# Hybrid decoder trunk on one core: three engines issue in the order of the text through the whole program instead of only in its first lines

## Chip, cores and metric

The kernel runs on one core of a Trainium2 chip. A core has a matrix engine (TensorE, PE in the profile), a vector engine (VectorE, DVE), a scalar engine (ScalarE, ACT), GpSimd (POOL) and SyncE (SP). Each takes its instructions from a queue of its own, in order, and they wait for one another by semaphores. In this kernel SP and POOL issue the DMAs. The metric is the device time of one execution in microseconds (us).

## Reference

One layer of a decoder trunk with two recurrent mixers beside each other, all in float32, for 1024 tokens of width 1024:

```python
mod = silu(c) @ ada_w + ada_b
shift, scale, gate = split(mod, 3)
h = rms_norm(x, norm_w) * (1 + scale) + shift
hq, hf, hi, hz, gq, gk, gv, gz, ga, mg = split(h @ w_in, IN_OFFSETS)
y_h = hgrn2_branch(hq, hf, hi, hz, lb, hgrn_norm_w)   # 8 heads, keys 128, values 128
y_g = gla_branch(gq, gk, gv, gz, ga, alpha_w, alpha_b, gla_norm_w)  # 4 heads, keys 128, values 256
mg = sigmoid(mg.reshape(B, T, 2, 1024))
merged = mg[:, :, 0] * (y_h @ w_branch[0]) + mg[:, :, 1] * (y_g @ w_branch[1])
x = x + gate * (merged @ w_out)
return rms_norm(x, final_norm_w)
```

Both mixers are gated linear attention: a state S of keys by values follows S_t = diag(a_t) S_(t-1) + k_t v_t^T, and the output is o_t = S_t^T q_t; the decay a_t is a gate of its own for each key channel. It is computed chunk by chunk: products of queries and keys inside a chunk, weighted by the decay between them, and the state between chunks. The GLA branch then takes a root mean square of each head, the HGRN branch one over all heads.

## The kernel before

All large products are made in three parts. A float32 operand is split into a rounded part `hi` (ScalarE, L193) and the remainder `lo` (VectorE, L196, for some GpSimd), and the product is hi·hi + lo·hi + hi·lo. Buffers in SBUF come from 46 slots of 128x1024 floats that the host hands out and takes back in a fixed order when it builds the program; PSUM has two double banks `pd`, one double bank `sc_ps` and two small banks `pm`.

The stages, in the order of the text:

- **Start.** `norm_x` (L204 to L208) normalizes the rows of x; TensorE transposes them (L215), ScalarE copies the result out (L217), and `make_h` (L224, then L193 and L196) applies shift and scale. Shift and scale come from `make_mod`, whose VectorE chains (L247, L251) and small products (L257, L259) read `ada_w` in five blocks. The first group of projections is made for the first half of the tokens while h comes out, one 128-row block `d` at a time (L349). Then the text has `make_ga` (L305), the eight transposes of the second half with their `make_h`, and `first_group`, which makes the second half's projections (L372).
- **Stream.** A list of projection jobs: `Feat` (L455, 48 products of 128x512 for 128 output features), `Vblk` and `Vblk2` (L514 to L516 and L557 to L559, values). Each job has a load (SP), a prep (the split of its weights, L193 and L196) and a run; its result leaves PSUM by a sigmoid and a product (L852, L853), by two sigmoids and three operations (L978 to L982) or by a copy (L519, L562). The class `Stream` calls a job's load and prep ahead of its run when slots are free.
- **Two tracks woven into the stream.** After every 6 products of a job, `weave` gives a bit of time to two queues of Python generators. The side track holds the attention of the heads, one after the other; the back track holds elementwise work for the last stages, mainly `weight_sums` (L1169 to L1173 with DMAs on POOL, L1175) and `factors` (L1138). A generator yields the number of 6-product units that should pass before its next step is put into the text. So the text is one sequence in which small steps alternate with groups of products.
- **Attention of a head** (`attention`, L571 on): builds of `xb` (ScalarE L589, VectorE L590 to L593); products of 16-wide pieces L597; VectorE L599 to L615, L624 and L625 with ScalarE L622 and L623; products L629; VectorE L631 to L635 and eight predicated copies L642 to L645; products L658, then VectorE L677, L678, L681, L684, and ScalarE L687; products L665, L677 and L678 again, ScalarE L692; products L671, L677 and L678, ScalarE L696; transposes L709, the states' products L731 with VectorE L737, the outputs' products L748 and L750. GLA heads close with `root_mean` (products L863 and L864, ScalarE L865) and, in four steps, a reciprocal L891 and two products L893 each.
- **Pair stage** (`last_stages`): four matrix products, each by seven products of half-size factors as in Strassen's scheme, for 4 groups b, in the order 1, 2, 5, 6, 3, 7, 4 of the products and over 4 `Pair` objects (L1293). Around them stand the splits of the weights (`prep_duo`, L1233 and L1234) and of the factors (`build`, L1211 to L1215), copies of a bank out of and back into PSUM (`snap_of` L1269 and L1271, `seed` L1276), sums (`summed`, L1280) and outputs.
- **Two output blocks** (L1076 to L1097).

What sets the order of issue: the text calls every instruction in one sequence, and dependences are turned into semaphores. Then a scheduler of the framework orders each engine's queue by its own model of the times, and it may put an instruction ahead of one that stands earlier in the text where no dependence forbids it. Within `tc.manual_schedule(engines=...)` the named engines keep the order of the text. The kernel opens this for PE, ScalarE and VectorE at L156 to L158, ahead of the first `vec_rows`:

```python
order = ExitStack()
order.enter_context(tc.manual_schedule(engines={
    mybir.EngineType.PE, mybir.EngineType.Activation, mybir.EngineType.DVE}))
vec_rows(rows_c, 8, R_C)
...
norm_x(0, x_t)
vec_rows(rows_a, 24, R_SH)
order.close()
make_mod(0, 1, mods.pop(0), 4)
```

It closes at L324, ahead of the first `make_mod`. Behind that line a handful of instructions are held by `tc.keep_in_program_order`, among them the first step of a `make_mod` chain and the first splits of the group's weights.

Of the kernel before, what the change touches and what calls it, by code (L numbers as in the profile page):

```python
# [83 lines left out]
def hybrid_trunk_kernel(  # L84
# [65 lines left out]
    def vec_rows(rows, n, at):  # L150
        pv = mtile()
        i = nc.tensor.transpose(pv[:, 0:n], rows, ident[0:n, 0:n])
        nc.vector.tensor_copy(vec[:, at:at + n], pv[:, 0:n])
        return i

    order = ExitStack()  # L156
# [84 lines left out]
    def make_mod(d0, nd, parts, on_pe):  # L241
        kq = 4 // nd
        acc = scT_f[:, (d0 // 2 % 2) * 512:(d0 // 2 % 2) * 512 + 2 * nd * P].rearrange("p (a f) -> p a f", a=2)
        for k in range(on_pe, KT):
            src = parts[k // kq][:, k % kq]
            if k == on_pe:
                i = nc.vector.tensor_scalar_mul(acc, src, cs[:, k:k + 1])  # L247
                if on_pe:
                    tc.keep_in_program_order(i)
            else:  # L250
                nc.vector.scalar_tensor_tensor(acc, src, cs[:, k:k + 1], acc, ALU.mult, ALU.add)  # L251
        pm = mtile()
        for half in range(2):
            for i in range(nd):
                o = pm[:, half * nd + i:half * nd + i + 1]
                for k in range(on_pe):
                    nc.tensor.matmul(o, parts[k // kq][:, k % kq, half, i * P:(i + 1) * P], cs[:, k:k + 1],  # L257
                                     start=(k == 0), stop=False)
                nc.tensor.matmul(o, acc[:, half, i * P:(i + 1) * P], one_t, start=(on_pe == 0), stop=True)  # L259
        S.free(*parts)  # L260
        nc.vector.tensor_add(modv[:, :, d0:d0 + nd], pm[:, 0:2 * nd].rearrange("p (a b) -> p a b", a=2),
                             vec[:, R_SH:R_SH + 16].rearrange("p (a b) -> p a b", a=2)[:, :, d0:d0 + nd])
        nc.vector.scalar_tensor_tensor(amul[:, d0:d0 + nd], modv[:, 1, d0:d0 + nd], 1.0,
                                       vec[:, R_NW + d0:R_NW + d0 + nd], ALU.add, ALU.mult)
# [56 lines left out]
        load_w(bi)  # L321
    norm_x(0, x_t)
    vec_rows(rows_a, 24, R_SH)
    order.close()  # L324
    make_mod(0, 1, mods.pop(0), 4)
    transpose_x(0, x_t, 0)
    transpose_x(0, x_t, 1)
# [1134 lines left out]
    make_m()  # L1462
    out0.run({1: out1.load, 3: out1.prep})
    out1.run({})


# [27 lines left out]
```

## Time and profile before

| | |
|---|---|
| runs | 1283.7, 1285.03, 1285.39 us |
| median | 1285.03 us |
| span of the profiled execution | 1279.6 us |
| TensorE busy | 1219.5 us (95%), 8603 instructions |
| VectorE busy | 802.6 us (63%), 1239 |
| ScalarE busy | 506.3 us (40%), 754 |
| GpSimd busy | 151.4 us (12%), 246 |

The profile gives the span from the first to the last instruction of the profiled execution; its time with what lies around the span is not given, and the median of the runs is 5.4 us above it. The page of the profile slices the span into 40 parts of 32 us with each engine's busy tenths; from the trace behind it come windows (busy time between two moments), groups of instructions by line, waits (which engine waited for what) and the timeline. A line such as `PE L455 MATMUL pd<-b,b` names the engine, the line of the text, the operation, what it writes and what it reads.

### The profile page before, as it was taken

Reading aid. Unit: us, or ns where it says so; the run is one execution under the profiler, and the core shown is the slowest. Engines: PE = TensorE matmul, PEld = TensorE weight load, DVE = VectorE, ACT = ScalarE, POOL = GpSimd, SP = SyncE. Lnnn points to the kernel's source line nnn. Section 1 sums busy time; section 2 is a strip of 40 time slices with the busy share of each in tenths; the row PEclk is TensorE's granted clock in tenths of the full one; section 3 lists DMA queues with packets and bytes.
Section 4 is the critical chain, followed back from the end, with each engine's and each line's share of the span. In section 5 each row is a group of like instructions: output and inputs, shape, how many; then the busy total and the mean of one; then the engine's idle time right before and its main releaser. Section 6 shows DMA issues by size and latency. Waiting matters only on the chain. (4 is left out here: it accounts for less than half of the span.)

```text
span 1279.6 us, 20905 instructions
## 1 busy us (share of the span) xinstructions
PE 1219.5 (95%) x8603; PEld 1002.3 (78%) x8603; DVE 802.6 (63%) x1239; ACT 506.3 (40%) x754; POOL 151.4 (12%) x246
## 2 busy tenths in 40 slices
PE   4899999999999999999999999999998999998997
PEld 3677899879797877787787878877786777776885
DVE  5746334785849475876874576686544555659643
ACT  4466612333333223323322233356544454364222
POOL 5510000101111121121220101011121000000000
PEclk9799999999999999999999999999999999999999
DMA  8733100654553266363272511336579846445402
GB/s 270 274 104 93 40 18 18 230 165 129 186 155 134 83 191 221 100 198 126 99 264 100 180 39 62 101 123 208 171 254 335 279 168 204 164 133 178 167 34 99
DMA packets 134129, 195.05 MB, mean 152 GB/s; under 512 B 7819, under 2 KB 97985, under 8 KB 134034
## 3 DMA queue, kind: packets, MB, share of 16 engines
q1 hardware_dynamic: 118114, 140.01, 34.9%
q0 software_dynamic: 15872, 53.70, 10.9%
q8 instruction: 67, 1.10, 0.3%
q14 instruction: 28, 0.23, 0.1%
q10 hardware_dynamic: 48, 0.01, 0.0%
HBM read 140.21 MB, written 53.48 MB: 151 GB/s over the span
## 5 line engine op out<-in xcount | busy, mean ns | idle before, releaser
L455 PE MATMUL pd<-b,b 128*128 128x512 f32 x1632 | 396.9, 397 | 0.0
L455 PEld LDWEIGHTS pd<-b,b 128*128 128x128 f32 x1632 | 301.1, 189 | 64.1 <-issue 1.2
L1293 PE MATMUL pd<-b,b 128*128 128x512 f32 x912 | 221.7, 395 | 12.6 <-ACT pd L1276 5.3
L1293 PEld LDWEIGHTS pd<-b,b 128*128 128x128 f32 x912 | 170.0, 189 | 55.0 <-ACT pd L1276 6.5
L196 DVE TENSOR_TENSOR b<-b,b 128x1024 fp32r<-128x1024 f32 (+1 forms) x95 | 101.0, 1072 | 69.4 <-ACT b L193 41.7
L193 ACT CAST b<-b 128x1024 fp32r<-128x1024 f32 (+1 forms) x95 | 84.6, 905 | 140.4 <-DMA ws<-b 16.8
L1293 PE MATMUL sc_ps<-b,b 128*128 128x512 f32 x432 | 108.6, 397 | 3.9 <-DVE b L1280 2.1
L1293 PEld LDWEIGHTS sc_ps<-b,b 128*128 128x128 f32 x432 | 81.2, 190 | 24.0 <-DVE b L1280 2.5
L1234 DVE TENSOR_TENSOR b<-b,b 128x1024 fp32r<-128x1024 f32 x56 | 68.0, 1222 | 45.3 <-ACT b L1233 28.6
L1233 ACT CAST b<-b 128x1024 fp32r<-128x1024 f32 x56 | 58.2, 1049 | 50.0 <-PE pd L1293 14.1
L514 PE MATMUL pd<-b,b 128*128 128x256 f32 x256 | 75.6, 295 | 0.0
L516 PE MATMUL pd<-b,b 128*128 128x256 f32 x256 | 72.5, 283 | 0.0
L515 PE MATMUL pd<-b,b 128*128 128x256 f32 x256 | 72.5, 283 | 0.0
L1175 POOL DMA_DIRECT2D ws<-b x64 | 35.3, 552 | 205.3 <-DVE b L1169 82.2
L1215 DVE TENSOR_TENSOR b<-b,b 128x1024 fp32r<-128x1024 f32 x36 | 43.4, 1220 | 25.5 <-ACT b L1214 14.1
L557 PE MATMUL pd<-b,b 128*128 128x512 f32 x128 | 51.9, 405 | 0.0
L1214 ACT CAST b<-b 128x1024 fp32r<-128x1024 f32 x36 | 37.6, 1050 | 35.2 <-PE pd L1293 10.0
L559 PE MATMUL pd<-b,b 128*128 128x512 f32 x128 | 50.2, 392 | 0.0
L558 PE MATMUL pd<-b,b 128*128 128x512 f32 x128 | 50.0, 390 | 0.0
L514 PEld LDWEIGHTS pd<-b,b 128*128 128x128 f32 x256 | 49.0, 191 | 0.5
L515 PEld LDWEIGHTS pd<-b,b 128*128 128x128 f32 x256 | 48.9, 191 | 0.6
L516 PEld LDWEIGHTS pd<-b,b 128*128 128x128 f32 x256 | 48.9, 191 | 0.0
(249 smaller groups left out, 1964.9 us busy)
## 6 DMA issues: line engine op xcount, KB each, us to landing
b<-in_w_in_dram SPq DMA_DIRECT2D x66, 512.0 KB, 4.0
ws<-b POOLq DMA_DIRECT2D x64, 256.0 KB, 3.1
b<-ws SPq DMA_DIRECT2D x32, 512.0 KB, 4.9
b<-in_x_dram SPq DMA_DIRECT2D x16, 512.0 KB, 6.7
b<-in_ada_w_dram SPq DMA_DIRECT2D x32, 256.0 KB, 6.0
b<-in_w_branch_dram SPq DMA_DIRECT2D x16, 512.0 KB, 4.8
b<-h SPq DMA_DIRECT2D x14, 512.0 KB, 4.3
b<-yg SPq DMA_DIRECT2D x14, 512.0 KB, 4.4
```

What stands on the lines that cost most here:

```text
L193: i = nc.scalar.copy(hi, src)
L196: (eng or nc.vector).tensor_sub(lo, src, hi.bitcast(F32))
L455: nc.tensor.matmul(ps[0:w, th * 512:(th + 1) * 512], a[:, k, 0:w], b[:, th * 512:(th + 1) * 512], start=(k == 0 and n == 0), stop=(k == KT ...
L514: nc.tensor.matmul(o, lh, hi[:, k % 4, :], start=(k == 0), stop=False)
L515: nc.tensor.matmul(o, lh, lo[:, k % 4, :], start=False, stop=False)
L516: nc.tensor.matmul(o, ll, hi[:, k % 4, :], start=False, stop=(k == KT - 1))
L557: nc.tensor.matmul(o, lh, hi[:, k % 2, :], start=(k == 0), stop=False)
L558: nc.tensor.matmul(o, lh, lo[:, k % 2, :], start=False, stop=False)
L559: nc.tensor.matmul(o, ll, hi[:, k % 2, :], start=False, stop=(k == KT - 1))
L1233: nc.scalar.copy(hi, t)
L1234: nc.vector.tensor_sub(lo, t, hi.bitcast(F32))
L1293: nc.tensor.matmul(o, a[:, sl], c, start=(p in (1, 5) and kt == 0 and n == 0), stop=(kt == 3 and n == 2), skip_group_check=True)
```

## The change

`order.close()` moves from L324 to the end of the kernel, behind the last output block. TensorE, VectorE and ScalarE then issue all their instructions in the order of the text; the queues of SP and POOL are still put in order by the scheduler. No instruction, buffer or dependence is added or taken away. Lines behind L324 have a number lower by one in the changed kernel.

```diff
     norm_x(0, x_t)
     vec_rows(rows_a, 24, R_SH)
-    order.close()
     make_mod(0, 1, mods.pop(0), 4)
     transpose_x(0, x_t, 0)
     transpose_x(0, x_t, 1)
...
     make_m()
     out0.run({1: out1.load, 3: out1.prep})
     out1.run({})
+    order.close()
```

## Prediction

> **What bounds the kernel now.** I read the page first, then windows by stage, TensorE's waits, and TensorE's timeline around the attention steps.
>
> ```profile
> span 1279.6 us, 20905 instructions
> PE 1219.5 (95%) x8603; PEld 1002.3 (78%) x8603; DVE 802.6 (63%) x1239; ACT 506.3 (40%) x754; POOL 151.4 (12%) x246
> PE   4899999999999999999999999999998999998997
> ```
>
> TensorE is busy in 1219.5 of 1279.6 us, so it is the bound, and no order of issue takes work off it: all that can be won is its idle time, 60 us, part of which is the start before any data is there. What can be lost has no such ceiling. The stages (start and end in us from the span's start, length, then busy time and instructions of PE, PEld, DVE, ACT and POOL, granted clock, DMA share, GB/s):
>
> ```profile
> 24.00:90.00 66.00, 58.85 (x254) 46.07 (x254) 41.80 (x63) 32.56 (x64) 25.26 (x28) 0.87 0.56 190
> 130.00:900.00 770.00, 756.82 (x6628) 635.73 (x6627) 515.30 (x857) 270.10 (x399) 93.36 (x127) 1.00 0.41 132
> 940.00:1185.00 245.00, 230.57 (x981) 184.36 (x981) 151.25 (x167) 119.64 (x158) 11.18 (x21) 0.99 0.64 214
> 470.00:485.00 15.00, 12.12 (x174) 9.55 (x174) 13.97 (x35) 3.25 (x4) 4.24 (x8) 1.00 0.62 209
> 584.11:587.52 3.41, 3.41 (x9) 2.64 (x10) 1.49 (x3) 0.67 (x1) 0.00 (x0) 0.50 0.32 86
> ```
>
> The 770 us from 130 to 900 hold the projections with the attention heads woven between them; TensorE idles there for 13.2 us in all. The pair stage (940 to 1185) idles for 14.4. VectorE has much to do beside both: 515 of 770 us, and 14.0 of 15 in the stretch at 470. So it has little slack where several of its pieces fall together.
>
> ```profile
> PE sc_ps L658 <- DVE blk L645: 6.8, 6, 2.5
> PE pd L1293 <- ACT pd L1276: 5.3, 3, 3.5
> PE pd L1293 <- DVE b L1234: 3.3, 2, 1.7
> ```
>
> These are TensorE's largest waits in those two stages (total, times, longest). In the attention they end on VectorE; in the pair stage on work that stands behind other work on ScalarE or VectorE.
>
> **The change part by part.** Nothing is added or removed: the same instructions, buffers and slots. Until now the scheduler brought each queue into an order of its own from the early lines on; afterwards PE, DVE and ACT follow the text, and only the DMA-issuing queues (SP, POOL) are still reordered. I matched the trace with the order in which the text calls the instructions. Some 650 of TensorE's 8603 records, 475 of ScalarE's and 885 of VectorE's come behind one that stands later in the text. So TensorE's queue is nearly the text's already (except for the attention's small steps, which the scheduler moved against the projection products), while VectorE's and ScalarE's are thoroughly different. What changes is that a DVE or ACT instruction that is ready no longer passes one that waits, and a split or a sum that is due much later stands where the text puts it, ahead of an attention step that TensorE will soon ask for.
>
> *Attention.* I walked the text head by head: how much TensorE work stands between one attention step and the next, and how much VectorE and ScalarE must do, in text order, in between. The fullest case is the last GLA head. First TensorE's present timeline (start, duration, line, count):
>
> ```profile
> 379.40 0.39 PE L864 MATMUL pm<-b,ones_r 128*128 128x512 f32 x1
> 383.95 8.38 PE L455 MATMUL pd<-b,b 128*128 128x512 f32 x36
> 392.26 1.31 PE L597 MATMUL sc_ps<-xb,b 128*32 128x80 f32 x64
> 393.51 7.09 PE L455 MATMUL pd<-b,b 128*128 128x512 f32 x30
> 400.53 0.89 PE L629 MATMUL sc_ps<-xb,b 128*32 128x48 f32 x64
> 401.35 4.37 PE L455 MATMUL pd<-b,b 128*128 128x512 f32 x18
> 406.35 0.73 PE L658 MATMUL sc_ps<-b,b 128*32 128x16 f32 x64 [0.63 <-DVE blk L645]
> ```
>
> Then the pieces of VectorE and ScalarE (busy, mean ns of one, idle before):
>
> ```profile
> L891 DVE RECIPROCAL b<-b 128x256 f32<-128x256 f32 x16 | 26.9, 1722 | 3.4 <-ACT b L865 3.4
> L893 DVE TENSOR_TENSOR b<-b,b 128x256 f32<-128x256 f32 x32 | 10.9, 403 | 0.0
> L1169 DVE TENSOR_TENSOR b<-b 128x512 f32<-128x512 f32 x16 | 11.0, 690 | 6.1 <-PE pm L748 2.8 <-PE pm L750 1.8 <-PE pd L455 0.9
> L591 DVE TENSOR_TENSOR xb<-b,b 128x512 f32<-128x512 f32 x12 | 13.4, 1119 | 0.0
> L593 DVE TENSOR_TENSOR xb<-xb,b 128x256 f32<-128x256 f32 x12 | 7.8, 649 | 0.1
> L853 DVE TENSOR_TENSOR b<-b,pd 128x1024 f32<-128x1024 f32 x24 | 29.4, 1223 | 11.9 <-ACT b L852 11.8
> L631 DVE TENSOR_TENSOR b<-xb,tot 128x768 f32<-128x768 f32 x12 | 12.0, 1001 | 0.0
> L644 DVE COPY_PREDICATED blk<-mask,sc_ps 128x64 f32<-128x64 int32 x24 | 5.5, 229 | 0.4
> L196 DVE TENSOR_TENSOR b<-b,b 128x1024 fp32r<-128x1024 f32 (+1 forms) x95 | 101.0, 1072 | 69.4 <-ACT b L193 41.7 <-PE pd L516 19.3 <-issue 3.2
> L677 DVE TENSOR_TENSOR b<-b,tot 128x512 f32<-128x512 f32 x36 | 24.8, 689 | 28.2 <-PE sc_ps L658 10.5 <-PE sc_ps L665 9.2 <-PE sc_ps L671 8.4
> L687 ACT COPY scT<-blk 32x256 f32<-32x256 f32 x48 | 19.3, 403 | 39.0 <-DVE blk L684 38.4
> L980 DVE TENSOR_SCALAR b<-b,oml,lb 128x1024 f32<-128x1024 f32 x8 | 6.5, 809 | 1.2 <-ACT b L978 1.1
> ```
>
> - At L597. Behind the root mean the text gives VectorE four reciprocals and eight products (4 x 1.72 + 8 x 0.40 = 10.1), four sums like L1169 (2.8) and the four builds L590 to L593 (between 0.65 and 1.12 each, 3.3): 16.2 us. TensorE arrives 12.9 us after the last L864 (392.26 less 379.40). The difference is 3.3; ScalarE's square root (L865) in front of the first reciprocal adds up to a microsecond, so 3 to 4.4, taken 3.9. Today the builds were done long before, ahead of the reciprocals.
> - At L629: 7.1 us of products against some 7.5 of VectorE: nothing.
> - At L658. VectorE has L853 (1.2), two sums (1.4), L631 to L635 (2.9: two of about 1.0, three small) and eight copies of about 0.2 (1.7): 7.2, against L629 and 18 products, 5.3: wait 1.3 to 2.3, taken 1.8.
> - At L665. Ahead of L677 the text has four splits L196 (4.3) and two sums (1.4); then L677 and its twin (1.4), two small ones (0.5), and ScalarE's four L687 (1.6): 9.2, against L658 and 18 products, 5.0: taken 4.2.
> - At L671. L980 to L982 stand ahead of the next L677 and wait for ScalarE's two gates behind the L687: some 5 us against L665 and 6 products (2.2): taken 2.7.
>
> Sum 12.6 for this head. The other GLA heads, walked alike: none for the first (nothing stands in front of it), 7 and 8 for the second and third (reciprocals and sums, but not the splits of a new block just there). The eight HGRN heads have no reciprocals; they wait where four splits of the next value block (4 x 1.07) fall between two steps, 5.1 and 3.3 in two heads, and 0 to 1.4 in the other six, 12.6 together. In all 12.6 + 15 + 12.6 = 40; the present idle of 13.2 is replaced, not added to: **+27**. Bounds: +5 (each wait shorter by about 1 us, of some 22) to +137 (all twelve heads like the fullest, 12 x 12.5 less 13.2).
>
> *Clock.* Behind the 2.5 us wait at L658 the clock stood at 0.50 for 3.41 us (window at 584.11); behind the two waits in the stretch at 470, which leave 2.9 us idle together, it stayed 1.00. A window costs 3.41 / 2 = 1.7 us. About ten of the walked waits are over 2 us: 17, of which half comes back because VectorE catches up meanwhile: **+9** (0 to 17). The Trainium skill ("TensorE: Matmul & The Clock Gate", section "HAM oscillation — how this bites in real kernels") warns of idle gaps over about 3.4 us; by it only some three of the walked waits would throttle, and this term would be near 5. The trace speaks for the lower threshold: its window at 584.11 stands behind a wait of 2.5 us.
>
> *Start.* The text makes all eight transposes of the second half ahead of the first-group products L372; today those products fill the gaps in which the transposes wait for ScalarE's copies:
>
> ```profile
> 84.68 1.66 PE L372 MATMUL pd<-b,b 128*128 128x512 f32 x6
> ...
> 91.56 2.58 PE L372 MATMUL pd<-b,b 128*128 128x512 f32 x10
> ...
> 85.25 0.57 ACT L217 COPY b<-pm 128x512 f32<-128x512 f32 x1
> 86.96 0.57 ACT L217 COPY b<-pm 128x512 f32<-128x512 f32 x1
> L251 DVE SCALAR_TENSOR_TENSOR scT<-b,cs,scT 128x512 f32<-128x512 f32 (+1 forms) x31 | 25.8, 861 | 0.5
> ```
>
> The copies come every 1.7 us; between the first and the last of those rows are five groups of six, five, six, five and ten products, about 7.3 us, of which I take 3.8 as lost for good (the rest is work TensorE would have had to wait for in either order) and one clock window, 1.7: 5.5. Make_mod's chains of eight L251 and one more (6.5 us for one block of weights) come between the product groups in text order; the first of them is earlier by about as much: +2.5. **+8** (-5 to +12, the 7.1 us that TensorE idles from 24 to 90 being the most that can be won there, and a chain more the most that is lost).
>
> *Pair stage.* Of 14.4 idle us the text removes those made by moving work forward: casts waiting for a weight that stand ahead of the seed L1276 (5.3), and part of L1234 (3.3). It brings back waits of a seed behind two factor builds:
>
> ```profile
> L1215 DVE TENSOR_TENSOR b<-b,b 128x1024 fp32r<-128x1024 f32 x36 | 43.4, 1220 | 25.5 <-ACT b L1214 14.1 <-PE pd L1293 5.2 <-issue 3.3
> ```
>
> Two builds are 2.4 us; I find 1.8, 0.6 and 0.7 of them uncovered in the first three groups. The last group stays bound by VectorE as it is. Net **-8** (-14.4, all idle time gone, to +8, a build's wait in each of the 28 product runs at 0.3 more). The output blocks at the end keep their order: 0.
>
> Sum: 27 + 9 + 8 - 8 = 36 (37 with its tenths). The profiled span of 1279.6 becomes 1316.6; the median of the runs lies 5.4 above the span (1285.03), so **1322**.
>
> **The rivals.**
> - *The scheduler's moves are what makes TensorE wait; the text's order is the smoother one.* For it: the pair stage's largest wait, 5.3 at L1276, is of that kind, and the weave gives every attention step 6 or more products of cover. Then attention waits stay under 1 us each and under the clock's threshold, some 13 in all as now, and the pair stage and its two clock windows go: 14.4 + 3.4 = 17.8 less, 1267. Against it: VectorE at 14.0 of 15 us at 470, and the count at L597 and L665, where the text asks for 16.2 and 9.2 us in 12.9 and 5.0. It decides if those counts are off by half. Chance 0.17; where only part of it comes true the time lies between 1267 and 1282.
> - *It compounds.* Every head is like the fullest one, because a late VectorE starts the next head late as well: +137 less the pair stage's 8, plus clock and start 17: 1430. For it: VectorE's 515 us in 770 leave it one third to catch up with; against it: that third lies in every head's last part (L709 to L750), where TensorE has long products and VectorE little. Chance 0.08.
> - *Almost nothing happens*, since TensorE's order is already the text's but for 650 records, and DMA queues are reordered in both: 1285. It would need VectorE to be ahead at each step. Chance 0.04.
> - The forecast: 0.71.
>
> **How the numbers follow.** About 0.2% (2.6 us) can be told from no change. Forecast's own range by the bounds of attention and clock: 1290 to 1370. Beside it stand the compounding case (above), and the two cases at or below 1285. The range 1270 to 1385 leaves out the fuller half of the faster rival and most of the compounding one. Slower: 0.71 + 0.08 and half of the third, 0.81; within 0.2%: 0.02; faster: 0.17. A result on the other side is most likely through start and pair stage together, whose lower ends (-5 and -14.4) with an attention term of +5 give 1271 to 1280.
>
> **What would show it.** In the profile after: TensorE's waits at L597, L658, L665 and L671 of the GLA heads on VectorE, together near 40 us (13 now) between 130 and 900; half-clock windows of 3.41 us behind those over 2 us, about ten; the copies' pitch of 1.7 us uncovered near 85; no wait at L1276 over 2 us. The same busy sums on every engine. It is wrong if VectorE never shows a reciprocal or a split as what ended a wait at an attention step, if the stretch 130 to 900 does not grow, or if the pair stage grows.

## The result

The changed kernel takes 1376.08 us (median of 4 runs, 1374.28 to 1378.59) against 1284.37 of the kernel before: a ratio of 1.0733, 95% interval 1.0701 to 1.0764. It is slower by 92 us, where 37 were forecast. The page of its profile, its span, the busy times, TensorE's busy tenths and its granted clock:

```profile
span 1376.9 us, 20896 instructions
PE 1243.6 (90%) x8603; PEld 1017.2 (74%) x8603; DVE 817.0 (59%) x1239; ACT 499.1 (36%) x750; POOL 144.3 (10%) x246
PE   4778999979888899999989999989899899997997
PEclk9888999999999999999999999999999999999999
```

The work is the same (8603 and 1239 instructions), yet TensorE's busy time is up by 24.1 us and its idle time from 60.1 to 133.3. The span is longer by 97.3: 73.2 of idle and 24.1 of longer products. The latter fits the clock, which is halved for 83 us of this trace and for 33 of the one before: 50 us more at half speed make 25. (The spans are of one execution each; that of before is 4.8 under the median of its runs, that of the changed kernel within 1 us of its own.) Windows by stage, cut where TensorE starts or ends a stage's products (first and last product of the first group's first half, last of its second half, first and last of the pair stage, end); first the kernel before, columns as in the prediction:

```profile
24.95:79.75 54.80, 49.40 (x196) 39.66 (x200) 37.27 (x55) 23.32 (x47) 24.16 (x26) 0.84 0.56 194
79.75:129.18 49.43, 48.52 (x222) 33.30 (x223) 28.22 (x45) 36.81 (x49) 2.17 (x4) 1.00 0.39 119
129.18:837.70 708.52, 698.11 (x6134) 589.36 (x6133) 469.00 (x795) 232.72 (x342) 87.41 (x120) 1.00 0.40 129
837.70:1183.00 345.30, 327.71 (x1641) 261.66 (x1640) 212.28 (x247) 175.50 (x241) 24.17 (x41) 0.99 0.61 202
1183.00:1279.60 96.60, 87.61 (x385) 71.53 (x383) 46.52 (x78) 26.56 (x56) 0.00 (x0) 0.97 0.27 102
```

The changed kernel, at the same places:

```profile
23.55:88.24 64.69, 50.48 (x196) 38.99 (x200) 38.86 (x61) 24.23 (x47) 21.88 (x26) 0.87 0.52 173
88.24:153.05 64.81, 54.00 (x223) 37.73 (x223) 20.53 (x35) 31.77 (x43) 2.17 (x4) 0.87 0.26 81
153.05:903.60 750.55, 709.91 (x6133) 597.23 (x6133) 482.23 (x796) 224.74 (x337) 83.19 (x120) 0.98 0.38 123
903.60:1276.50 372.90, 333.10 (x1640) 264.49 (x1638) 222.13 (x259) 180.86 (x247) 23.75 (x41) 0.98 0.57 190
1276.50:1376.90 100.40, 88.32 (x385) 71.77 (x384) 46.49 (x77) 26.05 (x55) 0.00 (x0) 0.98 0.23 86
```

Row by row: +9.9 in the first half of the start, +15.4 in its second half, +42.0 in the stream with the attention, +27.6 in the pair stage, +3.8 in the output blocks; less 1.4 because the first product comes earlier. The stream is near the forecast 36. Start and pair stage are not near 8 and -8.

**Stream.** TensorE's waits between 153 and 904 us of the changed kernel (total, times, longest):

```profile
PE sc_ps L670 <- DVE tot L680: 15.4, 6, 4.3
PE sc_ps L596 <- DVE xb L592: 12.2, 5, 4.5
PE sc_ps L657 <- DVE blk L644: 7.3, 5, 2.4
```

These are the steps that the prediction walked (L671, L597 and L658 there). The last GLA head on TensorE's timeline:

```profile
442.05 2.36 PE L596 MATMUL sc_ps<-xb,b 128*32 128x80 f32 x64 [4.53 <-DVE xb L592]
...
464.06 0.46 PE L664 MATMUL sc_ps<-b,b 128*32 128x32 f32 x32 [1.21 <-DVE blk L683]
...
470.32 0.69 PE L670 MATMUL sc_ps<-b,b 128*64 128x64 f32 x16 [4.22 <-DVE tot L680]
```

Ahead of the first stand reciprocals and sums on VectorE, as walked (wait 3.9 forecast). In front of the last stand ScalarE's two gates and VectorE's L979 to L981.

**First half of the start.** TensorE, then VectorE, of the changed kernel:

```profile
72.26 1.53 PE L348 MATMUL sc_ps<-b,b 128*128 128x512 f32 x6
73.63 0.95 PE L259 MATMUL pm<-ones,scT 128*128 128x1 f32 x8
77.05 0.49 PE L348 MATMUL pd<-b,b 128*128 128x512 f32 x1 [2.47 <-ACT b L193]
```

```profile
65.26 5.83 DVE L251 SCALAR_TENSOR_TENSOR scT<-b,cs,scT 128x512 f32<-128x512 f32 x7
74.62 0.16 DVE L261 TENSOR_TENSOR modv<-pm,vec 128x4 f32<-128x4 f32 x1 [3.53 <-PE pm L259]
```

VectorE's chain was done at 71.1. It is VectorE that then waits, for the eight small products L259, which TensorE reaches only at 73.63, behind the large ones of the row blocks in front. Only then can shift and scale (L261), h (L224) and its split (L193) follow, with nothing left for TensorE beside them. This repeats four times in the first half (at the second of them, TensorE also waits 2.1 us for VectorE's chain); between 23.55 and 88.24 TensorE idles 14.2 us.

**Pair stage.** Its groups begin at 903.6, 1012.1, 1099.3 and 1183.8 us. In the second group TensorE waits six times. Two of the waits are shown on its timeline, each with the run of twelve products in front:

```profile
1017.58 2.88 PE L1292 MATMUL pd<-b,b 128*128 128x512 f32 x12
1021.15 5.73 PE L1292 MATMUL pd<-b,b 128*128 128x512 f32 x24 [0.69 <-ACT b L1270]
...
1070.63 2.88 PE L1292 MATMUL sc_ps<-b,b 128*128 128x512 f32 x12
1077.52 4.56 PE L1292 MATMUL sc_ps<-b,b 128*128 128x512 f32 x12 [4.01 <-DVE b L1279]
```

What they wait for, on ScalarE and on VectorE:

```profile
1020.50 0.60 ACT L1270 ACTIVATE b<-pd 128x512 f32<-128x512 f32 x1 [1.19 <-PE pd L1292]
```

```profile
1069.20 2.47 DVE L1137 TENSOR_TENSOR b<-b,b 128x1024 f32<-128x1024 f32 x2
1071.60 0.68 DVE L1279 TENSOR_TENSOR b<-b,pd 128x512 f32<-128x512 f32 x1
1072.19 1.22 DVE L1137 TENSOR_TENSOR b<-b,b 128x1024 f32<-128x1024 f32 x1
...
1076.78 0.68 DVE L1279 TENSOR_TENSOR b<-sc_ps,b 128x512 f32<-128x512 f32 x1
```

The copy reads the half of a double bank that the run before has filled; the next run writes the other half of the same double bank, and the program lets it wait for the copy. At 1077 the reader is a sum on VectorE, with factors (L1137) and splits in front of it, and the wait is 4 us. The kernel before meets that second place like this:

```profile
993.07 2.88 PE L1293 MATMUL sc_ps<-b,b 128*128 128x512 f32 x12
995.79 2.20 PE L1293 MATMUL pd<-b,b 128*128 128x512 f32 x9
1000.08 4.61 PE L1293 MATMUL sc_ps<-b,b 128*128 128x512 f32 x12 [2.08 <-DVE b L1280]
```

Between the two runs on `sc_ps` the scheduler has put nine products of another run, and the wait is 2.08 us instead of 4.01.

### The profile page after: what moved, and what is told of

Same layout as the page of the kernel before. It is cut to its first block, busy times and chain, and to the rows that moved or that the text cites. A ratio compares the mean times of both kernels' runs of the same rounds, so it can differ in the third digit from the quotient of the medians.

```text
span 1376.9 us, 20896 instructions
## 1 busy us (share of the span) xinstructions
PE 1243.6 (90%) x8603; PEld 1017.2 (74%) x8603; DVE 817.0 (59%) x1239; ACT 499.1 (36%) x750; POOL 144.3 (10%) x246
## 4 chain that ended last, share of the span: by engine, by line
PE 65%; DVE 21%; ACT 6%; issue 5%; DMA 2%; POOL 1%; SPq 0%; DVEq 0%; ACTq 0%; POOLq 0%
PE pd L454 15%; PE pd L1292 11%; PE sc_ps L1292 4%; PE pd L371 3%; DVE b L196 2%; PE pd L556 2%; PE pd L513 2%; PE pd L557 2%; PE pd L515 2%; PE pd L514 2%; PE pd L558 2%; PE pm L747 2%; PE pd L348 2%; PE pm L749 2%; PE pm L730 2%
## 5 line engine op out<-in xcount | busy, mean ns | idle before, releaser
L454 PE MATMUL pd<-b,b 128*128 128x512 f32 x1632 | 403.1, 401 | 0.1
L454 PEld LDWEIGHTS pd<-b,b 128*128 128x128 f32 x1632 | 305.4, 191 | 66.4 <-issue 1.9
L1292 PE MATMUL pd<-b,b 128*128 128x512 f32 x912 | 225.1, 400 | 25.6 <-DVE b L1279 6.5
L1292 PEld LDWEIGHTS pd<-b,b 128*128 128x128 f32 x912 | 173.2, 192 | 70.4 <-ACT b L1270 8.2
L1292 PE MATMUL sc_ps<-b,b 128*128 128x512 f32 x432 | 106.9, 397 | 11.8 <-DVE b L1279 4.0
L1292 PEld LDWEIGHTS sc_ps<-b,b 128*128 128x128 f32 x432 | 81.2, 190 | 32.0 <-ACT sc_ps L1275 4.5
L193 ACT CAST b<-b 128x1024 fp32r<-128x1024 f32 (+1 forms) x95 | 83.9, 902 | 34.6 <-DVE b L1390 27.6
L686 ACT COPY scT<-blk 32x256 f32<-32x256 f32 x48 | 19.3, 403 | 112.2 <-DVE blk L683 111.8
L1232 ACT CAST b<-b 128x1024 fp32r<-128x1024 f32 x56 | 58.2, 1042 | 2.4 <-PE pd L1292 2.2
L556 PE MATMUL pd<-b,b 128*128 128x512 f32 x128 | 52.8, 413 | 0.0
L557 PE MATMUL pd<-b,b 128*128 128x512 f32 x128 | 50.7, 396 | 0.0
L558 PE MATMUL pd<-b,b 128*128 128x512 f32 x128 | 50.5, 394 | 0.0
L513 PEld LDWEIGHTS pd<-b,b 128*128 128x128 f32 x256 | 49.0, 191 | 0.5
L514 PEld LDWEIGHTS pd<-b,b 128*128 128x128 f32 x256 | 48.9, 191 | 0.4
L852 DVE TENSOR_TENSOR b<-b,pd 128x1024 f32<-128x1024 f32 x24 | 29.2, 1218 | 33.3 <-ACT b L851 33.2
```

Of the source, the lines that this page charges most:

```text
L193: i = nc.scalar.copy(hi, src)
L454: nc.tensor.matmul(ps[0:w, th * 512:(th + 1) * 512], a[:, k, 0:w], b[:, th * 512:(th + 1) * 512], start=(k == 0 and n == 0), stop=(k == KT ...
L513: nc.tensor.matmul(o, lh, hi[:, k % 4, :], start=(k == 0), stop=False)
L514: nc.tensor.matmul(o, lh, lo[:, k % 4, :], start=False, stop=False)
L556: nc.tensor.matmul(o, lh, hi[:, k % 2, :], start=(k == 0), stop=False)
L557: nc.tensor.matmul(o, lh, lo[:, k % 2, :], start=False, stop=False)
```

## The experiments

Two tables first. The times, all against runs of the kernel before on the same chip:

| run | us | ratio | 95% |
|---|---|---|---|
| e1_start | 1306.8 | 1.0220 | 1.0184 to 1.0257 |
| e2_stream | 1322.7 | 1.0347 | 1.0316 to 1.0377 |
| e3_last | 1308.4 | 1.0231 | 1.0202 to 1.0259 |
| e4_pe | 1347.6 | 1.0535 | 1.0504 to 1.0567 |
| e5_dve_act | 1310.5 | 1.0234 | 1.0199 to 1.0270 |
| e13_dve | 1293.9 | 1.0075 | 1.0054 to 1.0095 |
| e14_act | 1279.5 | 0.9964 | 0.9942 to 0.9986 |
| e6_lead | 1367.8 | 1.0678 | 1.0642 to 1.0714 |
| e9_half2 | 1374.6 | 1.0722 | 1.0704 to 1.0740 |
| e7_banks | 1350.8 | 1.0549 | 1.0506 to 1.0592 |
| e8_banks_before | 1271.4 | 0.9921 | 0.9886 to 0.9956 |
| e10_mid_two | 1259.1 | 0.9821 | 0.9801 to 0.9841 |
| e12_mid_three | 1265.0 | 0.9864 | 0.9845 to 0.9883 |
| e11_pool | 1407.5 | 1.0981 | 1.0960 to 1.1002 |
| e15_hold | 1378.5 | 1.0726 | 1.0688 to 1.0764 |

The stages in us, worked out from each trace by the same starts and ends of TensorE's products as above (start: up to the last L372):

| kernel | start | stream | pairs | output |
|---|---|---|---|---|
| before | 129.2 | 708.5 | 345.3 | 96.6 |
| changed | 153.1 | 750.6 | 372.9 | 100.3 |
| e1_start | 150.8 | 707.9 | 348.3 | 96.5 |
| e2_stream | 126.3 | 750.5 | 347.2 | 96.6 |
| e3_last | 126.9 | 710.8 | 368.1 | 100.7 |
| e4_pe | 149.7 | 720.7 | 372.8 | 100.5 |
| e5_dve_act | 135.9 | 724.5 | 354.7 | 96.2 |
| e13_dve | 134.6 | 716.2 | 345.5 | 96.2 |
| e14_act | 129.5 | 715.1 | 340.3 | 96.7 |
| e6_lead | 143.8 | 750.5 | 372.5 | 100.4 |
| e9_half2 | 144.7 | 753.8 | 372.9 | 100.3 |
| e7_banks | 151.3 | 750.5 | 352.1 | 94.8 |
| e8_banks_before | 126.1 | 709.1 | 337.4 | 93.6 |
| e10_mid_two | 127.4 | 709.6 | 328.6 | 93.6 |
| e12_mid_three | 129.0 | 707.5 | 330.5 | 93.7 |
| e11_pool | 149.0 | 783.7 | 372.5 | 100.3 |
| e15_hold | 152.1 | 750.1 | 375.2 | 100.5 |

### By stage

```diff
+ order = in_text_order(PE, Activation, DVE)   # e1: start; e2: First.run's end to last_stages; e3: last_stages to the end
  ...
+ order.close()                                # the scheduler orders everything else, as before
```

> Text order on the three engines through the start alone (up to the end of the first group of projections), the scheduler behind it. Theory A (each stage's loss is its own, and adds up): the 23.9 us by which the last L372 comes later in the changed kernel return here, the rest stays as before: 1308 us (1304 to 1312). Theory B (the prediction's price for the start was right and the rest came from a start that throws the later stages out of step): 1292 or less, or far more than 1312.

> Text order on the three engines only from the end of the first group to the head of the last stages (projections, attention, weight sums). Theory A: the 42.0 us between the last L372 and the first product of the pair stage: 1326 us (1320 to 1332). Theory B (attention waits come from what the start leaves late): under 1300.

> Text order on the three engines only from the head of the last stages on (pairs and output blocks). Theory A: 27.6 us of pairs and 3.8 of output blocks, less up to 6 that belong to the last attention head, which is still running there: 1310 us (1306 to 1317). The prediction's step on the pair stage (the text removes waits made by moving work forward): 1276.

The medians lie 26.5, 42.3 and 28.0 us over the shared median of before (1280.35), 96.8 in all, against 92 for the whole. Each run has nearly the changed kernel's time in its own stage and about the old one in the others. All three lie in the windows of theory A. So the losses are the stages' own and add up; a late start isn't carried along. The pair stage alone gets slower (368.1 against 345.3), which refutes the -8 by itself.

### By engine

```diff
- order.close()
+ order.close(); whole = in_text_order(PE)     # e5: DVE, Activation; e13: DVE; e14: Activation
  ...
+ whole.close()                                # behind the last output block
```

> Text order on TensorE alone through the whole program; VectorE and ScalarE by the scheduler. Theory C (the loss is VectorE's and ScalarE's head of line in start and attention; TensorE's own order matters only in the pair stage, where other products covered the copies out of PSUM): +10 to +30, 1295 to 1315, with TensorE's waits of 0.7 us on L1270, L1365 or L1370 there. Theory D (it is TensorE's order that loses the time everywhere): near 1376.

> Text order on VectorE and ScalarE through the whole program, TensorE by the scheduler: the counterpart of the run with TensorE alone, which lost 67 us (start 20.5, stream 12, pairs 27.5, output blocks 3.9). Theory E (TensorE's order makes the losses of start and pairs; in the stream it is VectorE's and ScalarE's order): start and last stages within 5 us of before, the stream +20 to +35, 1300 to 1320. Theory F (losses of start and pairs need only one of the engines in text order, whichever): start +15 or more and pairs +15 or more here too, 1340 or more.

> Text order on VectorE alone through the whole program. With VectorE and ScalarE together the stream lost 16 us, the start 6.7, the pairs 9.4. If VectorE's queue standing behind splits and reciprocals carries the stream's part: stream +10 to +16, whole 1300 to 1310. If it is ScalarE (small copies behind the first step of the splits): stream under +5, whole under 1295.

> Text order on ScalarE alone through the whole program. By the first reading above: stream under +5, and the waits of the pair stage on L1276 that come from casts put ahead of seeds gone (groups 1 and 2 at 80 to 83 and 77 to 79 us), whole 1278 to 1290. By the second: stream +10 to +16, 1295 to 1305.

Neither theory of the first holds: TensorE's order alone costs 67 us, not 10 to 30 and not the whole. Most of it (20.5, 27.5 and 3.9) lies in start, pairs and output blocks, nearly as much as the whole change loses there (23.9, 27.6, 3.8). VectorE's and ScalarE's order costs 6.7, 9.4 and nothing in these stages: theory E's 5 us are passed a little, theory F's 15 not reached. In the pair stage that 9.4 is a difference of two effects: the first and last group lose 10.9 and 8.0 us, the two between win 9.4. The stream is different: 12.2 for TensorE, 16.0 for the other two (theory E had 20 to 35), 42.0 for all three. There one free side makes up for a good part of the other's stiffness. So the losses of the engines don't add up as those of the stages do, and a share for each engine can't be read from them. With TensorE alone in text order most of its waiting in the stream is at one step (L664 there is L658 of the kernel before):

```profile
PE sc_ps L664 <- DVE blk L651: 16.2, 7, 6.1
```

VectorE alone costs the stream 7.7 and ScalarE alone 6.5, so neither expected reading of e13 and e14 holds: the 16 are shared. ScalarE in text order alone is a small gain in the times (ratio 0.9964, interval below 1), though its one trace does not show it (span 1281.6). In that trace the pair stage wins 5.0: its second and third group (groups 1 and 2 by the code's count) take 85.7 and 76.7 us against 87.9 and 81.2, where 80 to 83 and 77 to 79 were expected.

### The start

e6 works in the changed kernel. The text calls the next block's chain behind the current split, and its small products, shift, scale and h ahead of the current row block's large products:

```diff
+    prep(0)
     for d in range(KT):
-        make_mod(...)  # first d of a block
-        make_h(0, d); prep_wg(d, ...); transpose_x(0, x_t, d + 2)
+        if d + 1 in first: mod_end(*chain[0])      # L259, L261, L263 of the next block
+        prep(d + 1)   # make_h, prep_wg, transpose, then mod_chain (L247, L251) of the block after
         for f in range(NG):
             ...       # products L349 of d
```

> The changed kernel, with the text of the first half of the start turned round: the vector chain of the next block's shift and scale is called behind the current block's splits, and its small products, its shift and scale and the next row block's h ahead of the current row block's products. If the loss there is TensorE coming to the small products L259 only behind 24 large ones, so that L259, L261, L224, L193 and L196 stand in a row with nothing beside them (3.3 us four times, and the half clock behind each), the time from the first to the last L349 falls from 64.7 to 52 to 58 us, the whole to 1362 to 1370. If VectorE's chain itself is what is late, it stays at 62 or more.

The time from the first to the last L349 falls from 64.7 to 49.5 us, more than expected, partly because the first product now comes 6.9 later; the last L349 ends at 79.95 (88.24 in the changed kernel, 79.75 before). So the 9.9 of the first half are gone, and the time meets its window. The edit moves three things together, the chain, the small products and the next row block's h; that TensorE's late coming to L259 (behind the 18 products of one row block or the 36 of two, not 24) is all of the 9.9 is not shown. With TensorE alone in text order (e4) the first half takes 62.4 us, with VectorE and ScalarE alone (e5) 59.7, before 54.8. In e6 the chain is what is late, as its timeline shows (L262 here is L259):

```profile
64.95 1.07 PE L262 MATMUL pm<-ones,scT 128*128 128x1 f32 x8 [2.36 <-DVE scT L251]
```

e9 does the second half's first two outputs between the transposes:

```diff
     for d in range(KT):
         transpose_x(1, x_t2, d)
         make_h(1, d)
+        if d:
+            two(d - 1)          # six products of first_group's outputs 0 and 1
```

> The changed kernel with the text of the second half of the start turned round: behind each of the eight transposes the text makes the six products of the row block before for the first two of six outputs (as the scheduler did), instead of all eight transposes ahead of all products. If the loss from the last L349 to the last L372 (64.8 against 49.4 us) is transposes that wait for ScalarE's copies with nothing beside them, the half clock behind them and the first outputs' evictions behind eight splits, it falls to 50 to 56 us, the whole to 1362 to 1368. If it is the evictions alone (4.9 us of waits on L295 and L297), it stays over 60.

From the last L349 to the last L372 it takes 57.5 instead of 64.8 us: outside the expected 50 to 56, and 8.1 of the loss of 15.4 stay. The trace shows where: TensorE idles 6.5 us there (0.9 in the kernel before), and the other 2.5 are products at half clock. The largest wait is for an eviction of the first group (L384 here is L372):

```profile
PE pd L384 <- DVE b L295: 3.3, 1, 3.3
```

The same wait, 3.33 us, stands in the changed kernel, and VectorE's timeline there shows what stands in front. The eviction L295 comes behind steps of the side track (L830, L831) and a split, which stand ahead of it in the text:

```profile
115.30 1.22 DVE L196 TENSOR_TENSOR b<-b,b 128x1024 fp32r<-128x1024 f32 x1
116.44 0.68 DVE L295 TENSOR_SCALAR b<-pd 128x512 f32<-128x512 f32 x1
```

The stream gets longer by 3.2 at the same time, and the intervals of the two ratios overlap, so the gain isn't shown in the time, which misses its window as well.

### The pair stage

The order in which the host hands out the six halves of double banks can be followed in the code. It gives 26 places at which a run writes the other half of the double bank that the run before has just left to a reader. In the second group these are the second or fourth run in six of the seven products; the six waits of the trace stand at exactly these six runs. Three more lie in the output blocks. e7 and e8 choose the halves from a list; by the same count it has two such places (the expected text says six):

```diff
     def get(self, seeded=False):
-        fresh = [z for z in self.free_list if id(z) in self.fresh]
-        v = fresh[0] if fresh and not seeded else next(...)
+        v = self.named[PLAN.popleft()]   # B1 A0 B0 A1 s1 B1 s0 s0 B0 A1 ...
```

> The changed kernel with another choice of PSUM banks in the last stages: a fixed list in which the next run of products hardly ever writes the other half of the double bank that the copy, the sum or the output behind the last run still reads (6 such neighbours instead of 26, and none in the output blocks). If the waits of 0.69 us on L1270, L1268, L1365, L1370 and the 4 us ones on the sum L1279 come from sharing a double bank, the pair stage falls from 372.9 by 15 to 25 us and the output blocks by 3, the whole to 1348 to 1360. If they are a matter of VectorE's and ScalarE's backlog, the waits go to the run behind and the time stays over 1368.

> The kernel before with the same choice of banks. If the scheduler already covers the sharing by taking products of another run forward, little is left: 1274 to 1283. If the waits on L1276 and L1280 (5.3 and 2.1 us) come from sharing too, up to 9 us and two half-clock windows go: 1268.

In the changed kernel the pair stage falls by 20.8 and the output blocks by 5.5, and the ratio from 1.0733 to 1.0549; the whole, 1350.8 us, lies in its window. The groups of the stage (us from the first product of one to the first of the next, the last one to the end of the stage) show where:

| kernel | first | second | third | fourth |
|---|---|---|---|---|
| before | 93.7 | 87.9 | 81.2 | 82.5 |
| changed | 108.5 | 87.1 | 84.5 | 92.8 |
| e4_pe | 102.0 | 93.4 | 87.7 | 89.7 |
| e5_dve_act | 104.6 | 81.4 | 78.3 | 90.5 |
| e7_banks | 108.9 | 79.0 | 79.3 | 84.9 |
| e8_banks_before | 91.6 | 86.1 | 79.0 | 80.6 |
| e10_mid_two | 91.6 | 77.0 | 79.3 | 80.7 |

Sharing a double bank is the cause of waits in the last three groups, where the list takes off 8.1, 5.2 and 7.9 us. It is not the cause of the loss in the first group, 14.8 of the stage's 27.6: that one takes 108.9 us with the list too. The last attention head still runs there, and with the list TensorE waits 5.8 us at its steps (L596, L628, L657, L670), 3.9 for seeds and 2.1 for a gate's sigmoid. TensorE's order alone loses 8.3 us there, the other two engines' 10.9. Which waits make the 14.8 stays open. The Trainium skill ("PSUM — Partial Sum Buffer", section "The four PSUM rules") says that 512 float32 values fill one bank and that a product targets one bank only; by that, the two halves are separate memories and the wait would come from how the program tracks the tile. No run here reads the halves without that wait. The second and third groups take less time than with the scheduler. The largest waits that remain are seeds (ScalarE's L1283 here is L1276) and sums:

```profile
PE pd L1300 <- ACT pd L1283: 9.1, 6, 2.1
PE sc_ps L1300 <- DVE b L1287: 3.5, 2, 2.9
```

The kernel before gains too: 1271.4 us, 0.9921, between its two expected values. The scheduler had covered most, not all, of the sharing.

These two results point to a mixed version of the kernel before: the list, and text order in the second and third groups only.

```diff
+ if (b, p) == (1, 1): mid = in_text_order(DVE, Activation)   # e12: PE as well
+ if (b, p) == (3, 1): mid.close()
```

> The kernel before with the bank list and VectorE and ScalarE (not TensorE) in text order in groups 1 and 2 of the pair stage only. There the runs with text order took 81.4 and 78.3 us without the list, 79.0 and 79.3 with it and all three engines, the kernel before with the list 86.1 and 79.1. If the scheduler's moves on ScalarE and VectorE (casts put ahead of seeds) are what is left in group 1: 1262 to 1267. If the border between the orders costs as much: 1271.

> As the run before, with TensorE in text order too in groups 1 and 2: 79.0 and 79.3 us for these groups as in the changed kernel with the list, 1263 to 1268. If TensorE's freedom still covers something there, 2 us or more above the run with two engines.

e10 is faster than both kernels: 1259.1 us, ratio 0.9821, better than its window. The second group takes 77.0 us. TensorE's largest waits from 836 to 1250 us:

```profile
PE pd L1306 <- DVE b L858: 1.6, 1, 1.6
PE pd L1306 <- ACT pd L1289: 1.1, 1, 1.1
```

The wait on a seed (3.5 us before, 3.0 in e8) is gone. With TensorE in text order too (e12) the second group takes 79.0 and the whole 1265.0: TensorE's freedom is worth 2 us in that group. The medians differ by 5.9; the two traces don't show where the rest lies.

### The attention's waits

Two attempts to lighten VectorE's queue in the changed kernel missed. e11 puts the second step of the weight splits on GpSimd, e15 holds splits back while a head is between L645 and L671:

```diff
-        split(raw[:, :, 0:w], hi[...], lo[...])
+        split(raw[:, :, 0:w], hi[...], lo[...], nc.gpsimd)          # e11, also in Vblk and Vblk2
-        self.ahead(i, loads, preps)
+        self.ahead(i, loads, preps if last or not tight else 0)     # e15
```

> The changed kernel with the second step of the weight splits of all projection jobs (L196) on GpSimd in place of VectorE; ScalarE's first step (L193) stays where it is. If the waits at the attention steps come from VectorE's queue standing behind these splits, the stream falls from 750.5 by 12 to 25 us (1351 to 1364). If ScalarE's step in front of the small copies is as much to blame, by 3 to 10. If GpSimd is too slow for a job's weights, the stream gets longer.

> The changed kernel, with the splits of the next job's weights held back in the text while a head is between its copies L645 and its products L671, unless the job is in its last three steps. If the waits at L670 and L664 (15.4 and 1.2 us) come from these splits standing ahead of the attention's VectorE steps, they fall to under 8 us, the stream from 750.5 to 733 to 744, the whole to 1357 to 1370. If they only move to the products of the next job (waits of L454, L513 or L556 on L196), the time stays.

e11 is slower by 31 us, and the stream grows to 783.7. GpSimd takes 2.5 us for a subtraction that VectorE does in about 1.2 (L1215 of the prediction, the same shape):

```profile
L196 POOL TENSOR_TENSOR b<-b,b 128x1024 fp32r<-128x1024 f32 x50 | 126.4, 2535 | 290.3 <-ACT b L193 261.1 <-issue 29.0
```

That is not all. VectorE has 50 instructions fewer and is yet busy for longer, 834.0 us against 817.0, because its own instructions take longer beside GpSimd's:

```profile
462.47 8.18 DVE L630 TENSOR_TENSOR b<-xb,tot 128x768 f32<-128x768 f32 x1
462.83 7.01 POOL L196 TENSOR_TENSOR b<-b,b 128x1024 fp32r<-128x1024 f32 x3
```

L630 takes 0.95 us on average in the changed kernel. TensorE waits 7.8 us at the L657 that follows. In e11 44 of VectorE's instructions take at least 1.3 times and 0.3 us more than the median of their kind in the changed kernel; 41 of them overlap a GpSimd subtraction, and together they take 85 us more. So e11 doesn't test what a VectorE queue without the splits would give.

e15 leaves the stream as it is, 750.1. The wait on L670 (L672 here) is spread differently, hardly smaller:

```profile
PE sc_ps L672 <- DVE tot L682: 14.1, 8, 4.2
```

The second head's part shortens from 81.0 to 77.0 us, the first one's grows by 3.4. The waits don't move to the next job's products, as the other reading had it, but to other attention steps; that the splits held back stand in front of these is likely, not shown. So it stays open which pieces of VectorE's queue cost the stream how much. Shown is that both sides' order matters there, and that holding the splits back in this way doesn't help.

## Why the prediction was wrong in size

Direction and the stage with the largest loss were right; the time lies in the stated range, but the change is 92 us and not 37. Attention and clock, 36 of the forecast, came to 42; the rest of the miss is start, pair stage and output blocks. Of the signs of being wrong that the prediction names, one came true: the pair stage grew. Step by step:

- **Attention, +27: right, 30.2.** TensorE's idle time in the stream rises from 10.4 to 40.6 us. The second, third and fourth GLA heads wait 10.0, 8.5 and 10.0 (forecast 7, 8, 12.6). Single waits of the last GLA head are off: at L597 4.5 (3.9), at L658 none (1.8), at L665 1.2 (4.2), at L671 4.2 (2.7). So the sum is right in part by luck, as errors cancel. The HGRN heads up to the eleventh in order wait 12.2 (12.6 for all eight). The last runs beside the first pairs and waits 1.4 at a step of its own; 6.0 more are pair products that wait for ScalarE to read a bank. The compounding rival did not come: the ninth to eleventh head wait at most 0.7 us, so what the earlier ones lose doesn't build up.
- **Clock, +9: 11.8, with the price right and the threshold wrong.** Eight half-clock windows of 3.41 us lie in the stream, where there was one; at about 1.7 us each, seven more make 11.9. The prediction goes by the length of a wait, but that alone does not decide:

```profile
593.34 0.74 PE L657 MATMUL sc_ps<-b,b 128*32 128x16 f32 x64 [2.09 <-DVE blk L644]
...
387.11 0.69 PE L670 MATMUL sc_ps<-b,b 128*64 128x64 f32 x16 [3.18 <-DVE tot L680]
```

The clock is halved behind the wait of 2.09 us and not behind the one of 3.18. In this trace all half-clock stretches begin on one grid of 3.41 us: the starts in the stream (279.92, 307.23, 361.84, 440.35, 471.07, 593.95 and 692.93) lie whole multiples of it apart. Four stretches of this grid:

```profile
382.32:385.73 3.41, 1.61 (x9) 1.00 (x6) 2.39 (x4) 3.35 (x7) 0.27 (x1) 1.00 0.00 0
385.73:389.14 3.41, 2.03 (x22) 1.75 (x23) 3.38 (x7) 1.27 (x3) 1.81 (x4) 1.00 0.45 171
590.54:593.95 3.41, 1.32 (x68) 0.86 (x66) 3.17 (x12) 0.00 (x0) 0.00 (x0) 1.00 1.02 381
593.95:597.36 3.41, 3.41 (x22) 2.71 (x11) 2.05 (x5) 1.29 (x4) 0.00 (x0) 0.50 0.05 17
```

  The grid cuts the wait of 3.18 in two, 1.80 and 1.38 us of idle time; the 2.09 lies in one stretch, and the next stretch is at half clock. From 31 us on, each of the 17 full-clock stretches of this trace in which TensorE idles 1.89 us or more is followed by half clock, and none of the 352 with 1.84 or less. In the 17 traces together no stretch with 1.95 us or more is followed by full clock; 12 with less than 1.7, ten of them in the first 56 us, are followed by half clock, for which these traces show no reason. So where a wait falls on the grid decides whether it costs nothing, one half-clock stretch or, as with the 4.53 us at 442, two. That the term came out near 9 is partly luck: none of the half that it expected back is seen. The Trainium skill's figure of 3.4 us ("TensorE: Matmul & The Clock Gate", section "HAM oscillation — how this bites in real kernels") doesn't agree with this trace, which halves the clock behind 2.09.
- **Start, +8: mis-sized, 23.9.** The step that failed is make_mod's +2.5. It costed VectorE's chain and set an earlier beginning against it, and left out that the chain's end is eight small products in TensorE's own queue, behind 18 or 36 large ones (9.9; e6 takes it back). The second half's 5.5 was 15.4: the transposes' waits for copies, taken as 3.8, are 5.5, as the prediction had it, but evictions of the first group (4.9, not in its sum; the largest behind the side track's VectorE steps) and the clock (5.5 against 1.7) come on top. e9 takes back 7.3.
- **Pair stage, -8: wrong sign, +27.6.** The step that failed is "of 14.4 idle us the text removes those made by moving work forward". It counted what the scheduler's moves cost and not what they covered: the scheduler had TensorE take products of another run while a reader was still on the double bank. That did not show in the waits of before, just because it was covered. The list of halves, which removes most such places, gives back 20.8 us. Of the first group's 14.8, where the prediction found 1.8, it gives back nothing, and the cause there stays open. Nor does the -8 follow from its own pieces: 5.3 and at most 3.3 removed and 3.1 brought back make -5.5, unless the stage's two clock windows are counted too.
- **Output blocks, 0: +3.8**, for the same reason (e7: 94.8, with the list).
- Behind both stands one inference of the prediction: that TensorE's queue was nearly the text's, since only some 650 of 8603 records were moved. TensorE's order alone costs 67 us. Few moves, at the right places, are worth much.
- The faster rival's mechanism is real in the second and third groups, and worth about 9 us there (e5: 9.4 without the list; e10 against e8: 8.8 with it); the prediction took it for the whole stage.
- Two smaller slips: the terms 27, 9, 8 and -8 add up to 36, not 37, and the upper bound of 1370 is not what the bounds of attention (+137) and clock (+17) give.

## To carry to other kernels

A trace shows the waits that are there, not those that a reordering covers: before an order is fixed, look up for each moved instruction what stood in the text between its neighbours, above all on the engine that sets the time. A small product that opens a chain on other engines is called ahead of the large ones, and a buffer of two halves is handed out so that neighbours in time don't share it; with both in the text, less is left for a scheduler to cover. Text order by stage and by engine costs a few lines to try, and the best version here has both kinds of order.

## What the runs showed of the hardware

In the changed kernel's trace TensorE's clock is halved for whole stretches of a fixed 3.41 us grid: behind each full-clock stretch with 1.89 us or more of idle time from 31 us on, and behind none with 1.84 or less. A wait of 3.18 us that the grid cuts in two cost no clock, one of 2.09 within a stretch did. In e11 VectorE's L630 took 8.18 us beside three GpSimd subtractions, against 0.95 on average without them. GpSimd took 2535 ns for the float32 subtraction of 128x1024 in e11, about 2.1 times VectorE's 1.22 us for the same shape; the Trainium skill ("GPSIMD Engine Reference", section "3.1 Elementwise — side-by-side cycle accounting") gives 1.96 for an addition.
